# Cached sample keys of the third head group copied once through memory into 4 KB rows, and their reads issued from GpSimd

## The chip, the core and the metric

The kernel runs on one core of a Trainium2 chip. A core has a matrix engine (TensorE, PE in the profile), a vector engine (VectorE, DVE), a scalar engine (ScalarE, ACT), a general engine (GpSimd, POOL) and a queue engine (SyncE, SP) that mostly issues DMAs. Sixteen DMA engines move data between memory (HBM) and the on-chip memory. Each engine works through its own list of instructions in order and waits at semaphores. An instruction of one engine that has to wait holds up everything behind it on that engine, and nothing else.

The metric is the device time of one execution in microseconds (us). Lower is better.

## What is computed

One step of a decoder layer, for a prompt of 1024 tokens and for a sample group of 8 sequences with 8 new tokens each. The rest of the reference is a pooling branch, gates and a feed-forward part; the change concerns the attention of the sample tokens in the third of three head groups:

```python
ATTN_PATTERNS = ((128, 1), (512, 4), (2048, 16))     # (window, dilation) of the three groups of 4 heads
...
def dilated_attention_sample(q, k_full, v_full, dil, band):
    B, T, H, Dh = q.shape
    Lw = k_full.shape[1] - T
    idx = Lw + jnp.arange(T)[:, None] - jnp.arange(band + 1)[None, :] * dil
    valid = idx >= 0
    idxc = jnp.maximum(idx, 0)
    kg = k_full[:, idxc].astype(F32)
    vg = v_full[:, idxc].astype(F32)
    s = jnp.einsum('bthd,btjhd->bthj', q.astype(F32), kg) * (HEAD_DIM ** -0.5)
    p, lse = masked_softmax_stats(s, valid[None, :, None, :])
    return jnp.einsum('bthj,btjhd->bthd', p, vg), lse
```

With a dilation of 16 and 8 new tokens no two tokens of a sequence share a key. So each of the 64 sample tokens has 128 keys and values of its own in the cache, 16 rows apart.

## The kernel before

Products run in PE's passes over operands split into a high and a low part. Attention goes through the head groups in the order 2, 1, 0 (the third group first), and each group through 9 blocks: 8 of the prompt (0 to 7) and one of the sample tokens (8). For each block `qkv_part` multiplies the normed input by the weights of q, k and v. The order of PE's instructions is written out by hand; the order of the other engines' instructions is made by a scheduler that plays the program through with times of its own. `behind_pe` adds a wait on a product of PE, so that an instruction doesn't start ahead of its turn.

The norm of q and k of a block goes through four engines. ACT squares the product (L643 or L647), DVE or ACT sums the squares into `ms`, POOL adds a small constant (L650) and raises to the power -0.5 (L651, the result is `mr`), and ACT scales q and k by `mr` (L656, in `scale`). A few parts later PE transposes what was scaled (L672; the transposes are called `tqg2b`, `tqg1b`, `tqg0b` by the group). `smg0b` and its like are the scores, whose exponentials ACT takes in L699.

The own keys and values of the third group are not worked on by PE. `sample_own_keys` is a generator that takes one step with most parts of groups 1 and 0 (`own_step`). Its 128 partitions are the 64 sample tokens, twice: the first half of the 128 keys of each token in partitions 0 to 63, the second half in 64 to 127. It goes through 16 pieces of keys (`pck`) and then 16 of values (`pcv`); a piece has KPC = 4 keys of each partition, 512 KB. For a piece of keys POOL multiplies by the scaled q (`times`, L856, four instructions), and DVE sums over the head dimension into `sc` (L869). After the last one the softmax weights are made, and for a piece of values POOL multiplies by the weights and DVE adds the piece into `ss` (L894, L895).

Pieces are fetched by `piece` (L846): two DMAs of 64 partitions, each with 64 x 4 rows of 1 KB out of the cache. SP issues them. There are two buffers, so the DMA of the next piece but one waits until DVE has summed up the piece that holds its buffer. Every `times` waits also for PE's last product and for the last `mr` that was issued, so that a norm isn't queued behind it in the scheduler's order.

## Time and profile before

| | us |
|---|---|
| median of 3 timed runs | 1408.12 (1403.95 to 1409.54) |
| profiled execution | 1403.42 |
| its span, first to last instruction | 1401.6 |
| waits of POOL for key pieces (pck) | 24.5 in 10 |
| waits of POOL for value pieces (pcv) | 9.2 in 3 |
| POOL's products of key pieces, 64 | 47.4 |

The profile is of one execution. An engine's busy time is the time in which it had an instruction at work; its idle time is put down to what ended it. A share of 99% for PE says that the other engines cost time only where they make PE wait. In rows of the timeline the first number is the start in us from the span's start, the second the duration, and the bracket at the end holds the idle time ahead of it and what ended that. "SPq" and "POOLq" are the instructions with which SP and POOL issue DMAs and wait.

### The profile page before, as it was taken

How to read it: one execution, taken by the hardware profiler on the slowest of the kernel's cores; microseconds unless marked ns; L12 is line 12 of the kernel's file. 1: busy time of each engine (PE TensorE's matmuls, PEld its weight loads, DVE VectorE, ACT ScalarE, POOL GpSimd, SP SyncE). 2: the span in 40 equal slices, each digit the busy share in tenths (PEclk: the TensorE clock that was granted, in tenths of full speed). 3: DMA queues.
4: the chain of work that ended last, by engine and by line, in shares of the span. 5: the costliest groups of instructions: out<-in, count | busy, mean ns of one | idle time of the engine just before them, and what ended most of it. 6: DMA issues, size and time to landing. Idle time of an engine off the chain costs nothing.

```text
span 1401.6 us, 29306 instructions
## 1 busy us (share of the span) xinstructions
PE 1392.2 (99%) x11101; PEld 1342.7 (96%) x11101; DVE 954.3 (68%) x1714; ACT 754.5 (54%) x1778; POOL 236.2 (17%) x330
## 2 busy tenths in 40 slices
PE   9999999999999999999999999999999999999998
PEld 8988977887999999999999999999999999999998
DVE  7788744776776767875568677665665686664565
ACT  8557766687765323563336455555554544444443
POOL 0722266475500000000010000000000000000100
PEclk9999999999999999999999999999999999999999
DMA  6322788745477767965368668856758987777684
GB/s 215 117 90 102 220 228 215 216 127 144 120 254 232 253 216 250 319 227 179 130 203 285 227 221 269 269 200 210 249 189 287 325 272 261 234 243 231 206 260 168
DMA packets 184540, 303.57 MB, mean 217 GB/s; under 512 B 26567, under 2 KB 90509, under 8 KB 182350
## 3 DMA queue, kind: packets, MB, share of 16 engines
q1 hardware_dynamic: 181326, 258.04, 58.4%
q0 software_dynamic: 3072, 43.65, 9.8%
q8 instruction: 87, 1.43, 0.4%
q14 instruction: 55, 0.45, 0.1%
HBM read 231.55 MB, written 113.73 MB: 246 GB/s over the span
## 4 chain that ended last, share of the span: by engine, by line
PE 93%; DMA 2%; POOL 2%; DVE 1%; ACT 1%; issue 0%; SPq 0%; DVEq 0%; POOLq 0%
PE pz L1297 24%; PE pd L2075 24%; PE pg L1297 12%; PE ph L200 7%; PE pqk L200 5%; PE pab L1297 5%; PE pv L200 4%; PE a L328 3%; PE pq L200 1%; PE pk L200 1%; POOL pcv L856 1%; PE sg0b L689 1%; PE pog0b L722 1%; PE tpg0b L708 1%; POOL mr L651 0%; DMA ts_d<-ts 0%
## 5 line engine op out<-in xcount | busy, mean ns | idle before, releaser
L2075 PE MATMUL pd<-places 128*128 128x272 f32 x2688 | 331.7, 287 | 0.0
L2075 PEld LDWEIGHTS pd<-places 128*128 128x128 f32 x2688 | 331.6, 188 | 0.0
L116 ACT ACTIVATE places<-raw_d 128x544 fp32r<-128x544 f32 (+1 forms) x176 | 110.7, 646 | 162.7 <-DMA raw_d<-z_d 51.4
L117 DVE TENSOR_TENSOR places<-raw_d,places 128x544 fp32r<-128x544 f32 (+1 forms) x176 | 122.6, 712 | 92.4 <-ACT places L116 90.6
L2115 POOL DMA_DIRECT2D out_kv_sample_dram<-in_cache_kv_dram x96 | 47.2, 492 | 790.7 <-ACT places L116 580.9
L1297 PE MATMUL pz<-act,places 128*128 128x280 f32 (+1 forms) x1080 | 139.4, 287 | 0.0
L1297 PEld LDWEIGHTS pz<-act,places 128*128 128x128 f32 x1080 | 135.9, 188 | 0.0
L200 PE MATMUL ph<-act,places 128*128 128x280 f32 (+1 forms) x768 | 96.6, 287 | 0.0
L200 PEld LDWEIGHTS ph<-act,places 128*128 128x128 f32 x768 | 96.0, 188 | 0.1
L1297 PE MATMUL pg<-act,places 128*128 128x264 f32 (+1 forms) x576 | 75.6, 288 | 0.0
L1297 PEld LDWEIGHTS pg<-act,places 128*128 128x128 f32 x576 | 72.6, 188 | 0.6 <-issue 0.3
L1297 PE MATMUL pz<-places,apart 128*128 128x264 f32 (+1 forms) x528 | 67.9, 287 | 0.0
L1297 PEld LDWEIGHTS pz<-places,apart 128*128 128x128 f32 x528 | 66.6, 188 | 0.0
L200 PE MATMUL pqk<-places,act 128*128 128x512 f32 x240 | 60.6, 402 | 0.6 <-ACT qk L656 0.6
L1297 PE MATMUL pz<-act,apart 128*128 128x264 f32 (+1 forms) x456 | 59.2, 287 | 0.0
L1297 PEld LDWEIGHTS pz<-act,apart 128*128 128x128 f32 x456 | 57.5, 188 | 0.3 <-ACT e L1862 0.2
L200 PEld LDWEIGHTS pqk<-places,act 128*128 128x128 f32 x240 | 44.7, 192 | 10.5 <-ACT qk L656 0.8
L651 POOL TENSOR_TENSOR mr<-ms,mhalf 128x4 f32<-128x4 f32 (+2 forms) x39 | 52.9, 1356 | 3.1
L856 POOL TENSOR_TENSOR pck<-pck,qs 128x256 f32<-128x256 f32 x64 | 47.4, 774 | 29.1 <-DMA pck<-in_cache_kv_dram 24.5
L328 PE MATMUL a<-act,places 128*128 128x384 f32 (+1 forms) x288 | 50.3, 332 | 0.9 <-ACT act L306 0.4
L1297 PE MATMUL pab<-ab,places 128*128 128x264 f32 (+1 forms) x384 | 50.4, 286 | 0.0
L328 PEld LDWEIGHTS a<-act,places 128*128 128x128 f32 x288 | 47.5, 188 | 2.8 <-ACT act L306 1.2
(435 smaller groups left out, 2789.3 us busy)
## 6 DMA issues: line engine op xcount, KB each, us to landing
out_kv_sample_dram<-in_cache_kv_dram POOLq DMA_DIRECT2D x72, 480.0 KB, 4.9
raw_d<-z_d SPq DMA_DIRECT2D x112, 272.0 KB
z_d<-t SPq DMA_DIRECT2D x80, 272.0 KB
raw_d<-in_w_down_dram SPq DMA_DIRECT2D x80, 256.0 KB
raw_u<-in_w_up_dram SPq DMA_DIRECT2D x64, 256.0 KB
raw_qkv<-in_w_in_dram SPq DMA_DIRECT2D x36, 256.0 KB
pck<-in_cache_kv_dram SPq DMA_DIRECT2D x32, 256.0 KB
pcv<-in_cache_kv_dram SPq DMA_DIRECT2D x32, 256.0 KB
```

What stands on the lines that cost most here:

```text
L116: ins = s_.activation(dst_hi, src, AF.Copy)
L117: v_.tensor_tensor(dst_lo, src, dst_hi.bitcast(F32), op=ALU.subtract)
L200: last_mm[0] = t_.matmul(out, lhs(a, k), rhs(b, k), start=(j == 0), stop=(j == len(terms) - 1))
L328: last_mm[0] = t_.matmul(pts[m][:, :n], wt[:, a, kk, m * P:(m + 1) * P], act4[b][kk][:, :, part4(c)], start=(p == 0 and kk == 0), stop=(p ...
L651: last_norm[0] = g_.tensor_tensor(r[:n, :H], ms[:n, :H], mhalf[:n, :H], op=ALU.pow)
L689: t_.matmul(sc[e][:, hp, j * P:(j + 1) * P], qT[rows, hp, :], kT[rows, 2 + hp, :], start=True, stop=True)
L708: t_.transpose(tp[:, hp * nk + j, :], sms[e][:, hp, j * P:(j + 1) * P], ident)
L722: t_.matmul(po[e * HD:(e + 1) * HD, hp, :], vr[:, h * HD:(h + 1) * HD], pTs[e][:, hp * nk + j, :], start=(j == 0), stop=(j == nk - 1))
L856: ins = g_.tensor_tensor(out, *others, op=ALU.mult)
L1297: last_mm[0] = t_.matmul(out[c], lhs(*term), rhs(*term, c), start=(first and n == 0), stop=(n == len(terms) - 1), skip_group_check=not first)
L2075: last_mm[0] = t_.matmul(outs(chain[t], Q)[c], A[:, a, t * P:(t + 1) * P], Z[:, b, c], start=(fresh and f == 0 and n == 0), stop=(f == NG ...
L2115: ins = g_.dma_start(d, a)
```

## The change

It has two parts. First, during group 2 the keys of the 16 pieces are copied from the cache into a new array in memory, `own_d`: one tile for a piece, in which each of the 128 partitions has its four keys in one row of 4 KB. `own_rows` is a generator that issues two DMAs for a tile, 64 x 4 rows of 1 KB each, with a wait on PE's last product ahead of the first; one tile follows each of the prompt blocks' parts in group 2. `piece` then reads a piece of keys with one DMA of 128 rows of 4 KB. Values are read from the cache as before. Second, all of these DMAs are issued by POOL, where SP issued the reads of pieces before.

```diff
+    own_d = [dp.tile([P, KPC * 256], F32, name=f"own_d{n}") for n in range(16)]
...
     def piece(kv, j, name):
         t = rr(sp1, [P, KPC, 256], F32, name=f"pc{name}", tag="pc", bufs=2)
         src = i["cache_kv3"]
+        if not kv:
+            g_.dma_start(t.rearrange("p n d -> p (n d)"), own_d[j // KPC])
+            return t
         for hf in range(2):
             a = bass.AP(tensor=src.tensor, offset=src.offset + (64 * hf + j) * DIL[2] * NB * 512 + kv * 256,
                         ap=[[512, NT * NB], [DIL[2] * NB * 512, KPC], [1, 256]])
-            dma(t[64 * hf:64 * hf + 64], a)
+            g_.dma_start(t[64 * hf:64 * hf + 64], a)
         return t
+
+    def own_rows():
+        src = i["cache_kv3"]
+        row = DIL[2] * NB * 512
+        for n in range(16):
+            for hf in range(2):
+                a = bass.AP(tensor=src.tensor, offset=src.offset + (64 * hf + n * KPC) * row,
+                            ap=[[512, NT * NB], [row, KPC], [1, 256]])
+                behind_pe(g_.dma_start(own_d[n][64 * hf:64 * hf + 64].rearrange("p (n d) -> p n d", n=KPC), a))
+            yield
+
+    own_moves = own_rows()
...
                     feed()
+                    if g == 2 and b < 8:
+                        next(own_moves, None)
```

PE's instructions keep their order. The scheduler gives POOL, ACT, DVE and SP another one.

The first place is POOL in group 2, at blocks 1 and 2. In a row stand the line, the operation, and what is written from what; `ms` and `mr` are the two steps of the norm. Before:

```order
L650 TENSOR_TENSOR ms_1_1_1020<-ms_1_1_1020,stats 128x8
L651 TENSOR_TENSOR mr_1_1_1021<-ms_1_1_1020,mhalf 128x8
L650 TENSOR_TENSOR ms_2_1_1149<-ms_2_1_1149,stats 128x8
L651 TENSOR_TENSOR mr_2_1_1150<-ms_2_1_1149,mhalf 128x8
L650 TENSOR_TENSOR ms_3_1_1291<-ms_3_1_1291,stats 128x8
```

POOL in group 2 with the change, the same blocks:

```order
L860 DMA own_d_101<-in_cache_kv_dram 256x1x256 x2
L860 DMA own_d_102<-in_cache_kv_dram 256x1x256 x2
L651 TENSOR_TENSOR ms_1_1_1042<-ms_1_1_1042,stats 128x8
L652 TENSOR_TENSOR mr_1_1_1043<-ms_1_1_1042,mhalf 128x8
L860 DMA own_d_103<-in_cache_kv_dram 256x1x256 x2
L860 DMA own_d_104<-in_cache_kv_dram 256x1x256 x2
L651 TENSOR_TENSOR ms_2_1_1175<-ms_2_1_1175,stats 128x8
```

Between two norms stand two pairs of DMAs now; the first pair of the two waits for the product of v, the second for that of q and k, whose norm follows.

The second place is POOL in group 0, around the norm of block 1. Before:

```order
L651 TENSOR_TENSOR mr_0_1_3856<-ms_0_1_3855,mhalf 128x4
L856 TENSOR_TENSOR pcv_3823<-pcv_3823,sc 128x256 x4
L856 TENSOR_TENSOR pcv_3868<-pcv_3868,sc 128x256 x4
L856 TENSOR_TENSOR pcv_3945<-pcv_3945,sc 128x256 x4
L650 TENSOR_TENSOR ms_1_1_4061<-ms_1_1_4061,stats 128x8
L651 TENSOR_TENSOR mr_1_1_4062<-ms_1_1_4061,mhalf 128x8
L856 TENSOR_TENSOR pcv_4042<-pcv_4042,sc 128x256 x4
L856 TENSOR_TENSOR pcv_4167<-pcv_4167,sc 128x256 x4
L650 TENSOR_TENSOR ms_2_1_4212<-ms_2_1_4212,stats 128x8
```

POOL in group 0 with the change, from the same norm of block 0 on:

```order
L652 TENSOR_TENSOR mr_0_1_3888<-ms_0_1_3887,mhalf 128x4
L872 TENSOR_TENSOR pcv_3855<-pcv_3855,sc 128x256 x4
L850 DMA pcv_3900<-in_cache_kv_dram 64x4x256 x2
L850 DMA pcv_3977<-in_cache_kv_dram 64x4x256 x2
L872 TENSOR_TENSOR pcv_3900<-pcv_3900,sc 128x256 x4
L872 TENSOR_TENSOR pcv_3977<-pcv_3977,sc 128x256 x4
L651 TENSOR_TENSOR ms_1_1_4093<-ms_1_1_4093,stats 128x8
L850 DMA pcv_4074<-in_cache_kv_dram 64x4x256 x2
L652 TENSOR_TENSOR mr_1_1_4094<-ms_1_1_4093,mhalf 128x8
L850 DMA pcv_4199<-in_cache_kv_dram 64x4x256 x2
L872 TENSOR_TENSOR pcv_4074<-pcv_4074,sc 128x256 x4
L872 TENSOR_TENSOR pcv_4199<-pcv_4199,sc 128x256 x4
```

Three pairs of reads have come in between the norm of block 0 and that of block 1, the last of them between the two steps of the norm. Each pair waits in POOL's queue for DVE to be done with the buffer. From block 2 on two pairs stand in each block.

The third place is POOL at the start of group 1, from the first products of keys (`pck`) to the norm of block 1. Before:

```order
L856 TENSOR_TENSOR pck_2073<-pck_2073,qs 128x256 x4
L650 TENSOR_TENSOR ms_8_1_2198<-ms_8_1_2198,stats 64x4
L651 TENSOR_TENSOR mr_8_1_2199<-ms_8_1_2198,mhalf 64x4
L650 TENSOR_TENSOR ms_0_1_2252<-ms_0_1_2252,stats 128x4
L651 TENSOR_TENSOR mr_0_1_2253<-ms_0_1_2252,mhalf 128x4
L856 TENSOR_TENSOR pck_2172<-pck_2172,qs 128x256 x4
L856 TENSOR_TENSOR pck_2264<-pck_2264,qs 128x256 x4
L856 TENSOR_TENSOR pck_2324<-pck_2324,qs 128x256 x4
L650 TENSOR_TENSOR ms_1_1_2447<-ms_1_1_2447,stats 128x8
L651 TENSOR_TENSOR mr_1_1_2448<-ms_1_1_2447,mhalf 128x8
```

POOL at the start of group 1 with the change, from the norm of block 8 on:

```order
L652 TENSOR_TENSOR mr_8_1_2245<-ms_8_1_2244,mhalf 64x4
L872 TENSOR_TENSOR pck_2121<-pck_2121,qs 128x256 x4
L651 TENSOR_TENSOR ms_0_1_2298<-ms_0_1_2298,stats 128x4
L652 TENSOR_TENSOR mr_0_1_2299<-ms_0_1_2298,mhalf 128x4
L872 TENSOR_TENSOR pck_2219<-pck_2219,qs 128x256 x2
L845 DMA pck_2310<-own_d_101 128x1024
L872 TENSOR_TENSOR pck_2219<-pck_2219,qs 128x256 x2
L872 TENSOR_TENSOR pck_2310<-pck_2310,qs 128x256 x4
L845 DMA pck_2369<-own_d_102 128x1024
L651 TENSOR_TENSOR ms_1_1_2490<-ms_1_1_2490,stats 128x8
L652 TENSOR_TENSOR mr_1_1_2491<-ms_1_1_2490,mhalf 128x8
```

The norm of block 8 has moved ahead of the first products, that of block 1 stands behind three pieces where it stood behind four, and two reads have come in.

On ACT the scaling of q and k of a block, which waits for `mr`, has moved back by a few instructions in most blocks; in block 1 of group 0 it stands behind the exponentials of `smg0b`, where it stood ahead of them.

## The prediction

> **What bounds the kernel now.** I read the page's busy times first, then the digits of the 40 slices, the chain, the windows of the three attention stages, and last the waits of TensorE (PE).
>
> ```profile
> span 1401.6 us, 29306 instructions
> PE 1392.2 (99%) x11101; PEld 1342.7 (96%) x11101; DVE 954.3 (68%) x1714; ACT 754.5 (54%) x1778; POOL 236.2 (17%) x330
> POOL 0722266475500000000010000000000000000100
> DMA  6322788745477767965368668856758987777684
> PE 93%; DMA 2%; POOL 2%; DVE 1%; ACT 1%; issue 0%; SPq 0%; DVEq 0%; POOLq 0%
> ```
>
> PE leaves 1401.6 - 1392.2 = 9.4 us of its span unused. GpSimd (POOL) looks idle at 17%, but its digits say that it works in slices 2 to 11 alone, at up to seven tenths, and those are the slices the change touches (a slice is 35 us). The three stages, group 2, group 1 and group 0 of the attention, in that order:
>
> ```profile
> core 0: us, PE busy (x) PEld busy (x) DVE busy (x) ACT busy (x) POOL busy (x), PEclk, DMA share, GB/s
> 60.00:155.00 95.00, 95.00 (x660) 83.53 (x658) 76.09 (x183) 63.49 (x332) 30.00 (x31) 1.00 0.35 115
> 155.00:283.00 128.00, 125.07 (x1076) 104.60 (x1075) 76.11 (x202) 82.53 (x306) 68.33 (x94) 1.00 0.84 219
> 283.00:380.00 97.00, 96.94 (x799) 84.03 (x798) 67.06 (x187) 76.11 (x250) 62.42 (x86) 1.00 0.47 125
> ...
> PE pog1b L722 <- ACT pTg1b L711: 1.9, 1, 1.9
> PE pqk L200 <- ACT qk L656: 0.6, 1, 0.6
> PE tpg2b L708 <- ACT smg2b L699: 0.3, 1, 0.3
> ```
>
> The first rows are the windows, the last three PE's waits between 60 and 400 us. PE is full in all three stages, and waits 2.8 us in all. So **the change can win 2.8 us at most**. It can lose much more, since POOL makes the norm factors (mr) from which ScalarE (ACT) scales q and k, and PE transposes what is scaled. How late mr may come is read from pairs of rows: end of the scaling, start of the transposes of the same block.
>
> ```profile
> 87.70 1.75 ACT L656 ACTIVATE qk<-pqk,mr 128x64 f32<-128x64 f32 x8 [0.40 <-POOL mr L651]
> 94.15 0.60 PE L672 MATMUL tqg2b<-cst,qk 128*128 128x128 f32 x4
> ...
> 194.15 1.75 ACT L656 ACTIVATE qk<-pqk,mr 128x64 f32<-128x64 f32 x8 [3.18 <-POOL mr L651]
> 198.30 0.60 PE L672 MATMUL tqg1b<-cst,qk 128*128 128x128 f32 x4
> ...
> 307.36 1.75 ACT L656 ACTIVATE qk<-pqk,mr 128x64 f32<-128x64 f32 x8 [3.09 <-POOL mr L651]
> 311.95 0.60 PE L672 MATMUL tqg0b<-cst,qk 128*128 128x128 f32 x4
> 316.78 1.75 ACT L656 ACTIVATE qk<-pqk,mr 128x64 f32<-128x64 f32 x8 [0.18 <-POOL mr L651]
> 324.07 0.60 PE L672 MATMUL tqg0b<-cst,qk 128*128 128x128 f32 x4
> 376.25 0.66 PE L672 MATMUL tqg0b<-cst,qk 128*128 128x128 f32 x4
> ```
>
> The slack is 94.15 - 89.45 = 4.7 us in group 2, 198.30 - 195.90 = 2.4 in block 1 of group 1, 311.95 - 309.11 = 2.8 in block 1 of group 0, and 324.07 - 318.53 = 5.5 in its block 2. Blocks of group 0 follow each other every (376.25 - 311.95) / 5 = 12.86 us.
>
> **The price of a DMA on POOL.** The trace has POOL DMAs of one kind, 16 long rows each, and SP's DMAs of many kinds.
>
> ```profile
> L2115 POOL DMA_DIRECT2D out_kv_sample_dram<-in_cache_kv_dram x96: 488/488/717, 454.9 to 1335.0; - x96
> DMA to landing us min/median/max: 2.9/4.6/8.3
> ...
> q0 software_dynamic: 3072, 43.65, 9.8%
> ...
> L846 SPq DMA_DIRECT2D pcv<-in_cache_kv_dram x32: 595/610/1452, 262.8 to 366.0; - x32
> ...
> 60.32 0.33 SPq L127 DMA_DIRECT2D raw_qkv<-in_w_in_dram  x1
> ```
>
> Lower end: 0.49 us, the POOL row as it is. Upper end: in proportion to packets. 3072 / 96 = 32 packets cost 0.49, and 256 rows are at least 256 packets, so 8 x 0.49 = 3.9 us. SP, which generates in another way, pays 0.61 for this very pattern and 0.33 for a plain one, 1.85 times; 0.49 x 1.85 = 0.90. I take **1.0 us** for 256 rows (nearest to SP's ratio, a little above it since POOL's row had only 16) and 0.7 for the 128 rows of a key piece, between 0.49 and 0.9. All of this is an estimate; the chances below carry its doubt.
>
> By the Trainium skill, "DMA: Bandwidth & Descriptors", section "Anatomy of one DMA — SWDGE (gpsimd) path", a lot of descriptors can be emitted before their number costs anything; the price would then stay at 0.49, the result of the first rival. No POOL DMA of many rows is in this trace, so nothing here bears it out or refutes it.
>
> **The change part by part.**
>
> *Moves to own_d, group 2.* 16 pairs, 32 DMAs, 32 us: POOL goes from 30 to 62 of 95. Each pair waits for the product whose norm comes next, and stands ahead of ms and mr.
>
> ```profile
> 83.31 0.22 ACT L647 ACTIVATE qk<-pqk 128x64 f32<-128x64 f32 x1 [2.13 <-PE pqk L200]
> ...
> 85.14 0.45 POOL L650 TENSOR_TENSOR ms<-ms,stats 128x8 f32<-128x8 f32 x1 [9.89 <-ACT qk L647]
> ```
>
> After the product ACT squares for 85.14 - 83.31 = 1.8 us before POOL can begin, and POOL idles 9.9 us until then. A pair of 2.0 us makes mr 0.2 late, of 4.7 allowed: **0**. At 3.9 it would be 6.0 late, 1.3 us a block. The transfers add 8.4 MB: at the 219 GB/s for a share of 0.84 of the second window that is 38 us at 0.84, or 0.34 of 95 us on top of 0.35. There is room.
>
> *Key reads, group 1.* 16 x 0.7 = 11 us: POOL goes to about 80 of 128. Two reads, 1.4 us, come ahead of mr of block 1, where 2.4 are allowed and one piece of four products less stands in front: **0**. SP loses 64 issues of 0.61 us, and waits that go with them; SP is not in the chain, so I credit nothing there. The 0.6 us wait for qk goes, because mr of block 8 now stands ahead of the first products: **-0.6** (0 to -2.8).
>
> *Value reads, group 0.* 14 of the 16 pairs fall behind 283 us: 28 us, POOL at 90 of 97. Here it gets tight.
>
> ```profile
> L856 POOL TENSOR_TENSOR pcv<-pcv,sc 128x256 f32<-128x256 f32 x64 | 42.5, 695 | 22.2 <-DMA pcv<-in_cache_kv_dram 9.2 <-DVE natt L601 3.0 <-PE pv L200 2.9
> ...
> 296.92 2.33 POOL L856 TENSOR_TENSOR pcv<-pcv,sc 128x256 f32<-128x256 f32 x4 [2.15 <-DVE sel L1227]
> 302.28 2.83 POOL L856 TENSOR_TENSOR pcv<-pcv,sc 128x256 f32<-128x256 f32 x4 [3.03 <-DVE natt L601]
> 305.06 0.20 POOL L650 TENSOR_TENSOR ms<-ms,stats 128x8 f32<-128x8 f32 x1
> 305.34 1.98 POOL L651 TENSOR_TENSOR mr<-ms,mhalf 128x8 f32<-128x8 f32 x1
> ...
> 312.94 1.26 SPq L846 DMA_DIRECT2D pcv<-in_cache_kv_dram  x2
> 317.71 2.33 POOL L856 TENSOR_TENSOR pcv<-pcv,sc 128x256 f32<-128x256 f32 x4 [0.96 <-DMA pcv<-in_cache_kv_dram]
> 318.28 1.27 SPq L846 DMA_DIRECT2D pcv<-in_cache_kv_dram  x2
> 324.52 2.49 POOL L856 TENSOR_TENSOR pcv<-pcv,sc 128x256 f32<-128x256 f32 x4 [4.49 <-DMA pcv<-in_cache_kv_dram]
> ```
>
> Block 1: three pairs, 6.0 us, now stand between mr of block 0 and mr of block 1 (the order's rows). POOL idled 2.15 + 3.03 = 5.2 us there. If all of it absorbs issues, mr is 0.8 late and the slack of 2.8 covers it; if none does, because each pair waits for VectorE (DVE) to have added up the piece that holds its buffer and the products then wait for the landing, it is 6.0 late and PE stands 3.2. I take the middle, **+1.6**.
>
> Blocks 2 to 6: two pairs a block. Data land some 4.25 us after the issue (314.20 to 317.71 is 3.5, 319.55 to 324.52 is 5.0). One round on POOL: pair 2.0, mr 1.7, pair 2.0, landing 0.55, products 2.35, landing 1.35, products 2.35, ms 0.2: 12.5 us against PE's 12.86: **0**, with 5.5 of slack behind it.
>
> Sum: 0 + 0 - 0.6 + 1.6 + 0 = **+1.0 us**. On the profiled execution, 1403.4 us (1.8 beyond its span), that makes 1404.4; the median of the three timed runs is 1408.1, 4.7 above that execution, and I forecast on it: **1409 us**.
>
> **Rivals.**
> 1. *Flat issue price.* At 0.49 us the three pairs ahead of mr are 3.0, less than the idle 5.2. No stall, and between 0.6 and 2.8 us are won: about **1407**.
> 2. *POOL becomes the bound, slower.* At 1.7 us a DMA, block 1 adds 6 x 0.7 = 4.2 to the stall, 5.8. The round becomes 6.8 + 1.7 + 2.35 + 1.9 + 2.35 + 0.2 = 15.3, 2.4 beyond PE's pace in each of five blocks, 12 less the slack of 5.5: 6.7. With -0.6 that is +12: **1420**. It decides from about 1.5 us a DMA, where the same sum gives 7. For it: POOL is already at 62 of 97, and each read makes norm and products wait in one queue behind DVE. Against: SP's ratio of 1.85 and the 12.5 of 12.86. At 3.9 us it would be some 80 us.
> 3. *DVE's copies hold the issue back.*
>
> ```profile
> 326.04 1.88 DVE L601 CAST natt<-act 128x256 fp32r<-128x256 f32 x4
> ```
>
> If a pair of each block had to wait out these copies, the round is 14.4 us: 1.5 over in five blocks less 5.5 is 2, and block 1 takes 1.9 more: +5, **1413**. In the trace POOL's products once began just as such copies ended (3.03), and no DMA fell beside them. The Trainium skill, "SBUF — State Buffer", section "SBUF: two separate sides", says that GpSimd cannot write descriptors while a DVE copy of this kind holds the shared port.
> 4. *It does not do what it says:* 4 KB rows shorten what POOL waits for keys, and that wait is not on PE's path. This is inside the forecast. A result faster by over 7 us would need most of PE's 9.4 idle us, of which 2.8 lie in these stages.
>
> **How the numbers follow.** Chances: the forecast 0.46, flat price 0.15, POOL as bound 0.28, copies 0.08, something faster that I don't see 0.03. 0.5% is 7 us, about what a measurement of this kernel can tell from no change. Beyond +7 fall the second rival, 0.06 of the forecast (its upper ends) and 0.02 of the copies: slower 0.36. Faster 0.03 + 0.01 = 0.04. Same 0.60. The range goes from 1402 (all of PE's 2.8 won on a low run) to 1424 (the second rival a little above 1.7 us); above it lies some 0.12.
>
> **What would show it.** POOL's DMA row with 256 packets, at 0.8 to 1.3 us, settles the price. POOL busy near 62, 80 and 90 in the three windows, and the pairs of scaling and transposes with slack left except in block 1 of group 0, show the sum right. PE waits for qk or smg0b of more than 3 us between 283 and 400 us, or blocks further apart than 12.86, show the second rival. Wrong would be my reading if PE lost time in group 2, where I see none, or if the value pieces came so late that DVE stood behind them ahead of the softmax masks.

## The result, and the profile after

The changed kernel takes 1416.94 us (median of 6 runs, 1415.47 to 1419.86) where the kernel before takes 1406.45 us in the runs beside it (6 runs, 1403.95 to 1409.54). The ratio is 1.0077, with a 95% interval of 1.0066 to 1.0088: slower by some 10.5 us. The prediction had 1409 us as the likeliest time and 1402 to 1424 as its range; "slower by over 0.5%" had 0.36. One of the six executions of a kernel below (the change with both orders put back) was a slow one, 1938 us at a mean clock of 0.65, and its ratio leaves it out.

From the page of the profile after, the lines that answer to those of before (span, busy time of each engine, chain):

```profile
span 1416.0 us, 29304 instructions
...
PE 1397.5 (99%) x11101; PEld 1345.5 (95%) x11101; DVE 965.4 (68%) x1714; ACT 752.5 (53%) x1778; POOL 281.8 (20%) x410
...
PE 85%; DMA 6%; POOL 3%; DVE 2%; issue 1%; ACT 1%; SPq 0%; DVEq 0%; POOLq 0%; ACTq 0%
```

PE's unused time rose from 9.4 us to 1416.0 - 1397.5 = 18.5, and its share of the chain fell from 93% to 85%; what came in are DMA, POOL and DVE. PE's busy time rose too, by 5.3 us for the same products. The spans are 14.4 us apart, 3.9 more than the medians, since the profiled execution of before is a short one; landmarks below are from the two profiles and add up to the 14.4.

The windows of the three stages after, with the columns as before (busy time of PE, PEld, DVE, ACT, POOL, then granted clock, DMA share, GB/s), and behind them PE's waits between 60 and 400 us (total, times, longest):

```profile
60.00:155.00 95.00, 93.10 (x638) 81.46 (x637) 74.52 (x177) 59.38 (x319) 44.63 (x62) 1.00 0.60 187
155.00:283.00 128.00, 122.44 (x1032) 101.85 (x1032) 75.00 (x196) 80.21 (x302) 78.32 (x110) 0.99 0.72 221
283.00:380.00 97.00, 92.93 (x737) 78.58 (x736) 67.56 (x175) 70.42 (x235) 74.67 (x106) 1.00 0.47 120
```

```profile
PE pog2b L723 <- ACT pTg2b L712: 2.7, 1, 2.7
PE sg0b L690 <- ACT pTg0b L712: 1.2, 1, 1.2
PE tqg0b L673 <- ACT qk L657: 1.2, 1, 1.2
PE sg0b L690 <- DVE p L988: 1.1, 1, 1.1
PE sg2b L690 <- DVE qkTg2b L676: 1.0, 1, 1.0
```

Every stage leaves PE 2 to 6 us idle, the largest wait being 2.7. POOL's busy time is below the forecast in group 2 and group 0 (44.6 and 74.7, forecast 62 and 90), and at it in group 1 (78.3, forecast 80), because its DMAs are cheaper than I took them to be:

```profile
L2133 POOL DMA_DIRECT2D out_kv_sample_dram<-in_cache_kv_dram x96 | 47.1, 491 | 794.0 <-ACT places L116 583.8 <-ACT gapart L116 105.6 <-ACT apart L116 104.5
L850 POOL DMA_DIRECT2D pcv<-in_cache_kv_dram x32 | 20.5, 641 | 9.2 <-DVE sc L885 7.4 <-DVE ss L911 1.0 <-DVE md L699 0.8
L860 POOL DMA_DIRECT2D own_d<-in_cache_kv_dram x32 | 19.6, 619 | 33.0 <-PE pqk L200 21.7 <-PE tqg2b L673 4.4 <-PE tpg2b L709 2.6
L845 POOL DMA_DIRECT2D pck<-own_d x16 | 9.5, 594 | 12.4 <-PE tpg2b L709 5.9 <-DVE sc L885 5.5 <-DVE p L988 1.0
```

In these groups of POOL's DMAs the second number behind the bar is the mean in ns: 491 for 16 rows, 594 for 128, 619 and 641 for 256. So a price near to the first rival's, and a time near to the second's.

### Where PE falls behind

The best ruler is PE's transposes `tqg2b`, `tqg1b` and `tqg0b`, which come in the same order in all kernels. The table has how much later than in the kernel before some of them start in each profile; its columns are named by the start in before (the first and one of the last in group 2; the first and the last of group 1; the first and the last of group 0), and the last one is the span. The difference of two neighbouring columns is what is lost on the way from one to the other. Each row is one profile. How far two executions of one kernel differ by it was not measured; but the five runs whose edit leaves group 2 to itself (issuer alone, all on SP, values held, price alone, norms in order) all lose 0.0 between the first two columns, so that part of the ruler repeats.

| profile | 83.11 | 142.64 | 182.81 | 279.63 | 296.00 | 386.98 | span |
|---|---|---|---|---|---|---|---|
| the change | 0.3 | 2.2 | 5.7 | 7.4 | 8.1 | 13.6 | 14.4 |
| moves alone | 0.2 | 2.2 | 7.9 | 6.4 | 6.4 | 6.2 | 7.8 |
| moves of one row alone | 0.4 | 2.7 | 3.5 | 4.3 | 4.3 | 4.0 | 5.8 |
| issuer alone | 0.0 | 0.0 | 6.3 | 5.4 | 6.2 | 10.9 | 10.8 |
| change, values on SP | 1.0 | 2.3 | 4.5 | 6.0 | 6.8 | 7.4 | 7.4 |
| all on SP | 0.0 | 0.0 | 5.5 | 3.3 | 3.3 | 3.6 | 5.0 |
| values held on SP | 1.1 | 1.1 | 2.9 | 4.1 | 4.1 | 21.4 | 21.1 |
| issue price alone | 0.2 | 0.2 | 0.4 | 5.4 | 5.4 | 7.9 | 8.6 |
| all on SP, norms in order | 0.6 | 0.6 | 3.4 | 0.8 | 1.0 | 1.4 | 1.0 |
| moves alone, both orders put back | 0.2 | 1.5 | 6.6 | 7.9 | 7.9 | 8.1 | 7.7 |
| change, both orders put back | 0.6 | 2.8 | 6.8 | 8.7 | 9.6 | 14.4 | 14.6 |
| the same, first keys on SP | 0.8 | 4.6 | 9.5 | 9.1 | 10.1 | 14.7 | 15.5 |
| all on SP, norms first | 0.2 | 1.0 | 1.2 | -1.3 | -1.3 | -0.9 | -0.2 |

The change loses 0.3 us ahead of group 2's first transposes, 1.8 in group 2, 3.5 at its end, 2.4 on the way through group 1 (1.7 of it up to the last transposes there), 5.5 in group 0 and 0.8 behind it: 14.4, but for rounding.

**The end of group 2.** Rows of the timeline after, by engine (start, duration, and in the bracket the idle time and what ended it), and then slices of 1 us with the granted clock as the third number from the right:

```profile
162.11 1.17 POOL L845 DMA_DIRECT2D pck<-own_d  x2 [5.89 <-PE tpg2b L709]
...
163.04 0.33 SPq L127 DMA_DIRECT2D raw_qkv<-in_w_in_dram  x1
...
169.54 0.63 ACT L116 ACTIVATE places<-raw_qkv 128x512 fp32r<-128x512 f32 x1 [6.09 <-DMA raw_qkv<-in_w_in_dram]
170.07 0.35 ACT L712 COPY pTg2b<-tpg2b 128x256 f32<-128x256 f32 x1
...
170.48 0.96 PE L723 MATMUL pog2b<-pTg2b,v 128*64 128x128 f32 x6 [2.70 <-ACT pTg2b L712]
```

```profile
170.00:171.00 1.00, 0.52 (x5) 0.52 (x6) 0.97 (x3) 0.96 (x4) 0.00 (x0) 0.84 1.02 421
171.00:172.00 1.00, 1.00 (x7) 0.67 (x5) 0.97 (x3) 0.00 (x0) 0.00 (x0) 0.50 1.01 387
172.00:173.00 1.00, 1.00 (x7) 1.00 (x6) 0.49 (x2) 0.80 (x3) 0.00 (x0) 0.50 1.06 384
173.00:174.00 1.00, 1.00 (x7) 1.00 (x7) 0.96 (x3) 1.00 (x5) 0.75 (x2) 0.50 1.12 396
```

In the kernel before the same places look like this in the timeline:

```profile
162.62 1.32 ACT L116 ACTIVATE places<-raw_qkv 128x512 fp32r<-128x512 f32 x2 [2.68 <-DMA raw_qkv<-in_w_in_dram]
...
166.96 1.32 SPq L846 DMA_DIRECT2D pck<-in_cache_kv_dram  x2
```

Before, the first reads of keys stood in SP's queue behind its last loads of weights (`raw_qkv`) and started at 166.96. POOL's queue has no such loads in it: it issues the two reads at 162.11, 1 MB, just ahead of the load of 163.04, which is the one that ACT takes up at 169.54 (loads and ACT's steps come in one order, and both are the 22nd of 36). From its issue until ACT goes on that load takes 6.5 us; before, the same load was issued at 158.66 and taken up at 162.62, 4.0 later. So it comes later for two reasons: 4.4 us by its issue, where PE itself is 2.9 behind, and 2.5 by its landing. ACT is 6.1 us idle, and the copy pTg2b that PE needs stands behind that on ACT. PE waits 2.7 us, and for 3.4 us after it (170.67 to 174.09) the granted clock is 0.5; by the slices that is 0.52 x 0.16 + 3 x 0.5 = 1.6 us of PE's work more.

The Trainium skill, "TensorE: Matmul & The Clock Gate", section "Part 1: The HAM clock gate (the "warmup" mystery)", puts PE's clock at one half after an idle window of about 3.4 us, and back at full after a busy one of that length. The trace agrees with the half and with the length of the way back; but a shorter idle time was enough here: 2.7 us, in 3.41 us before the drop of which PE was busy for 0.71.

**Group 0.** The longest round of value pieces after, from POOL's, DVE's, ACT's and PE's timelines:

```profile
327.06 1.25 POOL L850 DMA_DIRECT2D pcv<-in_cache_kv_dram  x2
328.33 1.67 POOL L652 TENSOR_TENSOR mr<-ms,mhalf 128x8 f32<-128x8 f32 x1
329.95 1.29 POOL L850 DMA_DIRECT2D pcv<-in_cache_kv_dram  x2
334.64 2.33 POOL L872 TENSOR_TENSOR pcv<-pcv,sc 128x256 f32<-128x256 f32 x4 [3.40 <-DMA pcv<-in_cache_kv_dram]
338.73 3.11 POOL L872 TENSOR_TENSOR pcv<-pcv,sc 128x256 f32<-128x256 f32 x4 [1.76 <-DMA pcv<-in_cache_kv_dram]
341.80 0.20 POOL L651 TENSOR_TENSOR ms<-ms,stats 128x8 f32<-128x8 f32 x1
...
337.01 0.69 DVE L910 TENSOR_TENSOR pcv<-pcv 128x512 f32<-128x512 f32 x1 [4.75 <-POOL pcv L872]
...
342.70 0.22 ACT L752 ACTIVATE ce<-ce 128x24 f32<-128x24 f32 x1 [4.57 <-DVE ce L751]
...
342.93 0.37 PE L690 MATMUL sg0b<-qkTg0b,qkTg0b 64*128 64x128 f32 x1 [1.09 <-DVE p L988]
```

The pair issued at 327.06 has landed by 334.64, 6.3 us after its issue ended at 328.31. That is not the common case: over the 32 value reads the median from issue to landing is 3.9 us, and these land late beside three loads of weights (`raw_ga`) that SP issues from 325.32, with the DMA share at 1.0 or more from 327 to 336 us. POOL's products wait for it, DVE stands 4.75 us behind the products to add the piece up, ACT stands 4.57 behind DVE, and PE waits for what DVE and ACT have left undone (`p`, pTg0b). The round takes 341.94 - 327.06 = 14.9 us where PE's pace is 12.86, and PE loses 1.7 us up to the next transposes.

The larger loss, 2.6 us between the transposes of blocks 4 and 5, comes in no long round (352.63 to 361.68) but again by order. Rows of after:

```profile
359.70 0.69 DVE L910 TENSOR_TENSOR pcv<-pcv 128x512 f32<-128x512 f32 x1 [3.72 <-POOL pcv L872]
...
361.50 0.51 ACT L700 ACTIVATE smg0b<-smg0b,md 128x256 f32<-128x256 f32 x1 [2.72 <-DVE md L699]
...
369.70 1.75 ACT L657 ACTIVATE qk<-pqk,mr 128x64 f32<-128x64 f32 x8 [2.07 <-POOL mr L652]
371.30 0.64 ACT L712 COPY pTg0b<-tpg0b 128x512 f32<-128x512 f32 x1
...
371.99 0.37 PE L690 MATMUL sg0b<-qkTg0b,qkTg0b 64*128 64x128 f32 x1 [1.20 <-ACT pTg0b L712]
```

DVE stands 3.7 us behind POOL's products ahead of the softmax masks (`md`), and ACT 2.7 behind the masks. Later POOL's mr comes late as well, ACT idles 2.1 us for it, and the copy pTg0b stands behind that scaling in ACT's order: PE waits 1.2 us. The products that PE makes meanwhile out of `natt`, which DVE and ACT copy, take 3.96 us where they took 3.05 before, 0.9 more.

### The profile page after: what moved, and what is told of

It reads as the page before. It is cut to its first block, busy times and chain, and to the rows that moved or that the text cites. A ratio compares the mean times of both kernels' runs of the same rounds, so it can differ in the third digit from the quotient of the medians.

```text
span 1416.0 us, 29304 instructions
## 1 busy us (share of the span) xinstructions
PE 1397.5 (99%) x11101; PEld 1345.5 (95%) x11101; DVE 965.4 (68%) x1714; ACT 752.5 (53%) x1778; POOL 281.8 (20%) x410
## 4 chain that ended last, share of the span: by engine, by line
PE 85%; DMA 6%; POOL 3%; DVE 2%; issue 1%; ACT 1%; SPq 0%; DVEq 0%; POOLq 0%; ACTq 0%
PE pd L2093 23%; PE pz L1315 22%; PE pg L1315 12%; PE ph L200 7%; PE pab L1315 5%; PE a L329 3%; PE pqk L200 2%; PE pv L200 2%; DMA pcv<-in_cache_kv_dram 2%; POOL pcv L872 2%; DMA ts_d<-ts 2%; PE pq L200 1%; DMA raw_qkv<-in_w_in_dram 1%; PE pk L200 1%; POOL mr L652 1%
## 5 line engine op out<-in xcount | busy, mean ns | idle before, releaser
L872 POOL TENSOR_TENSOR pck<-pck,qs 128x256 f32<-128x256 f32 x64 | 47.4, 771 | 16.2 <-DMA pck<-own_d 10.9
```

The lines of the kernel that those rows point to most:

```text
L872: ins = g_.tensor_tensor(out, *others, op=ALU.mult)
```

## The experiments

Each ratio is against the kernel before, with a 95% interval; 0.1% is 1.4 us.

### One part of the change at a time

Moves alone: `piece` reads from the cache by SP again.

```diff
-        if not kv:
-            g_.dma_start(t.rearrange("p n d -> p (n d)"), own_d[j // KPC])
-            return t
...
-            g_.dma_start(t[64 * hf:64 * hf + 64], a)
+            dma(t[64 * hf:64 * hf + 64], a)
```

> The moves to own_d stay (32 DMAs on POOL in group 2), but the pieces of keys and values are read from the cache by SP, as before; own_d is written and not read. Theory G (the loss has two places, and one is group 2: the moves, by their traffic or by their place in POOL's queue, make PE late): +4 to +7 us against before, with PE's last transposes of group 2 (tqg2b of block 7) 4 to 6 us later than before, and no further loss in groups 1 and 0. Theory V (the loss comes from reads on POOL's queue alone, and what is seen in group 2 is another order of work that is made up later): 0 to +2 us. My prediction's own step said 0.

Measured: 1.0052 (1.0034 to 1.0070). The loss in group 2 is there, 1.9 us between the first two columns, though not the 4 to 6 that I expected; then PE waits 4.8 us for qk at the start of group 1, which the change doesn't.

Issuer alone: the kernel before, with `g_.dma_start` for `dma` in `piece`, and no own_d.

> No own_d and no moves; the reads of keys and values come from the cache as before, in two DMAs of 1 KB rows each, but POOL issues them. Theory G: group 2 is as before to 0.5 us, and the loss is that of groups 1 and 0, +5 to +9 us, most of it in group 0. Theory V: +9 to +12 us, the whole loss. My prediction's own steps said +1.6 for value reads in block 1 of group 0 and 0 after it. The price of a DMA of 256 rows into on-chip memory should again be about 0.63 us.

Measured: 1.0052 (1.0032 to 1.0071). Group 2 is as before to 0.0, group 0 loses 10.9 - 6.2 = 4.7 us. Each part alone costs half a per cent, and the whole 0.77%: they don't add up, since at the start of group 1 each loses something in another way.

Values on SP: the change, with `dma` for the value reads alone.

> The change as it is, but the reads of values are issued by SP again; moves and key reads stay on POOL. Theory G: the loss of group 0 goes, that of group 2 stays: +4 to +7 us. Theory V: 0 to +2 us. If value reads aren't the cause in group 0: still +9 to +12.

Measured: 1.0050 (1.0033 to 1.0068). The loss of group 0 falls from 5.5 to 0.6 us.

All on SP: moves, key reads out of own_d and value reads issued by `dma`.

```diff
-            g_.dma_start(t.rearrange("p n d -> p (n d)"), own_d[j // KPC])
+            dma(t.rearrange("p n d -> p (n d)"), own_d[j // KPC])
...
-            g_.dma_start(t[64 * hf:64 * hf + 64], a)
+            dma(t[64 * hf:64 * hf + 64], a)
...
-                behind_pe(g_.dma_start(own_d[n][64 * hf:64 * hf + 64].rearrange("p (n d) -> p n d", n=KPC), a))
+                behind_pe(dma(own_d[n][64 * hf:64 * hf + 64].rearrange("p (n d) -> p n d", n=KPC), a))
```

> The layout of the change with SP as the issuer of everything: the moves, the reads of keys out of own_d and the reads of values. The traffic is that of the change, POOL's queue is that of before. If the loss in group 2 is traffic: +4 to +7 us, with PE's last transposes of group 2 late by 4 to 6. If it is the place of the moves in POOL's queue: within 1.5 us of before, unless SP's own queue, which issues 32 DMAs more at some 0.6 us and waits for PE ahead of them, holds up the loads and stores of group 2; then the waits for raw_qkv and ts_d show that.

Measured: 1.0015 (1.0000 to 1.0030). With the same traffic group 2 loses nothing (0.0). PE has one large wait, at the start of group 1, and the rows of POOL's timeline say why:

```profile
PE pqk L200 <- ACT qk L657: 4.6, 1, 4.6
```

```profile
175.60 2.81 POOL L872 TENSOR_TENSOR pck<-pck,qs 128x256 f32<-128x256 f32 x4 [4.80 <-DVE sc L890]
178.36 0.34 POOL L651 TENSOR_TENSOR ms<-ms,stats 128x4 f32<-128x4 f32 x2
178.66 1.98 POOL L652 TENSOR_TENSOR mr<-ms,mhalf 128x4 f32<-128x4 f32 x2
```

POOL stands in the first key products, and the two norms behind them (of blocks 8 and 0) have come out in another order: block 0's mr is first, and ACT scales block 8, for which PE waits, after block 0 and two exponentials.

### What it is in group 2 and in group 0

Moves of one row, each DMA cut from 64 partitions to 1:

```diff
-                            ap=[[512, NT * NB], [row, KPC], [1, 256]])
-                behind_pe(g_.dma_start(own_d[n][64 * hf:64 * hf + 64].rearrange("p (n d) -> p n d", n=KPC), a))
+                            ap=[[512, 1], [row, KPC], [1, 256]])
+                behind_pe(g_.dma_start(own_d[n][64 * hf:64 * hf + 1].rearrange("p (n d) -> p n d", n=KPC), a))
```

> As the run with the moves alone, but each move copies one partition of its 64 (4 rows of 1 KB), so own_d stays mostly unwritten; it isn't read. 32 DMAs are still issued by POOL at the same places, with the same waits for PE, at some 0.49 us each where they took 0.6; nearly all traffic is gone. Theory T (the traffic, set off by POOL just ahead of the stores of ts, lands on the same DMA engines and holds those stores up, and DVE waits for them): ts_d lands within 3.5 us again, DVE's wait for it falls from 9.3 to about 4 us, and PE's transposes of group 2, blocks 2 to 6, are at most 0.5 us later than before, where they were 2.2 with the full moves. Theory P (the place in POOL's queue, in front of the norm): still 2 us late. In total, the wait of 4.8 us for qk at the start of group 1, which I put down to another order of two norms, should stay: +4 to +6 by T, +7 by P.

Measured: 1.0027 (1.0010 to 1.0044). Nearly all traffic is gone, and group 2 loses 2.3 us, no less than with it. Theory T falls. The wait for qk at the start of group 1, which I expected to stay at 4.8 us, is 0.9 here: such waits come and go with the scheduler's order. Four rows cost POOL 549 ns in the mean of 32 DMAs (median 520).

Values held: the kernel before, with each value read on SP waiting for the last product of the piece ahead (`piece` gives its two DMAs a wait on `last`).

```diff
-            if j + KPC < 64:
-                loaded.append(piece(1, j + KPC, f"v{j + KPC}"))
             for n in range(KPC):
                 tv = t[:, n].rearrange("p (h d) -> p h d", h=4)
-                times(tv, tv, sc[:, j + n, :].unsqueeze(2).to_broadcast([P, 4, HD]))
+                last = times(tv, tv, sc[:, j + n, :].unsqueeze(2).to_broadcast([P, 4, HD]))
+            if j + KPC < 64:
+                loaded.append(piece(1, j + KPC, f"v{j + KPC}", last))
```

> The kernel before, with value reads on SP, each held until POOL's products of the piece ahead of it are done, as POOL's own order holds them in the change. POOL issues nothing. Theory O (order: what costs time in group 0 is that a read issued by POOL starts only after POOL's next products, some 2 us after its buffer came free, so that the piece lands late, POOL's products are late, and DVE and ACT, in their order, after them): blocks of group 0 further apart, +3 to +6 us between the first and the last transposes of group 0 against before, and about that in total. Theory P (the time in which POOL issues, 1.25 us a pair, ahead of mr): 0 to +1 us.

Measured: 1.0117 (1.0088 to 1.0147), 17.3 us of it in group 0, with two stretches there in which PE's clock is at one half. Reads that start later cost PE time with POOL issuing nothing, but far more than the change loses: a read held on SP also holds what stands behind it in SP's queue. The sign speaks for theory O, the size can't be used.

Price alone: two DMAs more on POOL for each value piece.

```diff
                 loaded.append(piece(1, j + KPC, f"v{j + KPC}"))
+                for hf in range(2):
+                    a = bass.AP(tensor=i["cache_kv3"].tensor, offset=i["cache_kv3"].offset + (64 * hf + j) * DIL[2] * NB * 512,
+                                ap=[[512, 1], [DIL[2] * NB * 512, KPC], [1, 256]])
+                    ins = g_.dma_start(own_x[j // KPC, hf:hf + 1].rearrange("p (n d) -> p n d", n=KPC), a)
+                    behind_pe(ins, adds[-1] if adds else None)
```

> The kernel before, with value reads on SP as before, and with two more DMAs on POOL for each value piece, each of one partition (4 rows of 1 KB) into an array that nothing reads. They wait for DVE's sum as a read would, and stand in POOL's order where the change has its reads. They take POOL 2 x 0.49 us, most of the 1.25 us of a real pair, and add hardly any traffic. Theory P: +3 to +6 us in group 0. Theory O: 0 to +1.5 us. If both come to about half, the loss is the sum of the two.

Measured: 1.0025 (1.0009 to 1.0041), 2.5 us of it between the first and the last transposes of group 0 (a wait of 3.8 us for pTg1b at the end of group 1 costs more, and the change doesn't have it). So about half of the 4.6 to 5.5 us of the four profiles with value reads on POOL is the time and the place of the issue; the other half, by subtraction alone, comes with the reads themselves.

### Orders put back

Norms in order: all on SP, and each ms waits for the mr before it.

```diff
-            g_.tensor_tensor(ms[:n, :H], ms[:n, :H], xeps[go][:n, col:col + 1].to_broadcast([n, H]), op=ALU.add)
+            ins = g_.tensor_tensor(ms[:n, :H], ms[:n, :H], xeps[go][:n, col:col + 1].to_broadcast([n, H]), op=ALU.add)
+            if last_norm[0] is not None:
+                behind_pe(ins, last_norm[0])
```

> As the run with everything on SP, with one wait more: POOL's step ms of each norm waits for the mr before it, so that the norms stay in the order of the kernel before. At the start of group 1 that puts the norm of block 8 ahead of that of block 0 again, where the scheduler had let both ms go first. If the 4.6 us that PE waited there for qk, and the stretch after it in which the granted clock was 0.5, come from that order: the wait falls to 1 us or less, no stretch of lower clock is left, and the time falls by 4 to 6 us, to 2 us below before. If they come from something else (keys landing late, SP's queue): no change against that run, +2 to +3 over before.

Measured: 0.9989 (0.9972 to 1.0006), 2.6 permille below the run without it. The wait fell from 4.6 to 2.4 us, not to 1, and a stretch of some 3 us at a clock near 0.5 stayed: block 8's norm is first now, but still behind key products that wait for their DMA.

Both orders put back: the wait above, and DVE's window sum `win` (L477) waiting for the last sum of `ts` (L533) ahead of it in the program; for the moves alone, and for the whole change.

```diff
-                v_.tensor_tensor(v[:, 2], v[:, 2], v[:, 0], op=ALU.add)
+                last_ts[0] = v_.tensor_tensor(v[:, 2], v[:, 2], v[:, 0], op=ALU.add)
...
-            behind_pe(v_.tensor_tensor(nxt[:, lo:], cur[:, lo:], cur[:, lo - w:LS - w], op=ALU.add))
+            ins = v_.tensor_tensor(nxt[:, lo:], cur[:, lo:], cur[:, lo - w:LS - w], op=ALU.add)
+            behind_pe(ins)
+            if last_ts[0] is not None:
+                behind_pe(ins, last_ts[0])
```

> The moves alone (all of their traffic, issued by POOL in group 2; pieces read from the cache by SP), with two orders put back to those of the kernel before by waits of an engine on itself: DVE's window sums (win) wait for the last sum of ts that stands ahead of them in the program, and POOL's ms waits for the mr before it. The run with the moves cut to one row had lost as much in group 2 as the full moves, so traffic is not the cause there. Theory S (the scheduler's other order of DVE, which puts the store of ts 2 to 3 us later, is the cause): blocks 2 to 6 of group 2 at most 0.7 us later than before, where they were 2.2; the wait for qk at the start of group 1 at 1 us or less; in total 0 to +2.5 us where the moves alone had +7. Theory P (POOL's issue ahead of the norm is the cause): still 2 us late in group 2, +3 to +4 in total.

> The change as it is, with the same two orders put back. By S, what is lost in blocks 2 to 6 of group 2 goes (2.2 us), and what is left is the wait of 2.7 us for pTg2b with its stretch at half clock, and the loss of group 0 (5.5 us): +6 to +9 us against before, where the change had +10.5. By P: still +10 to +11.

Measured: 1.0051 (1.0035 to 1.0066) for the moves alone, 1.0094 (1.0074 to 1.0114) for the change. Neither gains. In group 2 (between the first two columns) the moves on POOL lose 1.3 us where they lost 1.9, but the wait on `ts` has a cost of its own there: with all on SP and both orders put back (the last run below) group 2 loses 0.8 us. With DVE's order put back POOL's moves thus lose 0.5 more than SP's, without it 1.9 more. That points to the order, and isn't clean enough to call it shown: the whole change with both orders put back loses 2.2 there.

First keys on SP: the change with both orders put back, and the first two key pieces read by SP.

```diff
-            g_.dma_start(t.rearrange("p n d -> p (n d)"), own_d[j // KPC])
+            (dma if j < 2 * KPC else g_.dma_start)(t.rearrange("p n d -> p (n d)"), own_d[j // KPC])
```

> As the change with the two orders put back, but SP issues the first two reads of keys, behind its loads of raw_qkv. Theory C (collision: POOL's queue lets these two reads of 512 KB start at 162 us, beside the loads of raw_qkv, which land 3 us later; ACT waits for them 6 us, PE for ACT 2.7, and the clock falls to a half): PE's wait for pTg2b goes, ACT's longest wait for raw_qkv falls from 6 to about 3 us, 3 to 5 us less than the run beside it that keeps these reads on POOL. If the late loads come from something else (their own issue, the moves): no difference to that run.

Measured: 1.0080 (1.0066 to 1.0095), no clear gain on the run beside it. In ACT's and PE's waits (ACT's between 150 and 190 us):

```profile
ACT places L116 <- DMA raw_qkv<-in_w_in_dram: 6.8, 5, 2.9
ACT qk L662 <- DVE sc L890: 2.8, 1, 2.8
```

```profile
PE pqk L200 <- ACT qk L662: 2.6, 1, 2.6
```

The collision is gone as theory C has it: ACT's longest wait for raw_qkv is 2.9 us where it was 5.7 in the run beside it, the load that took 6.2 us from issue until ACT goes on in that run takes 3.3, and PE's wait for pTg2b isn't there. But keys that are read later land later, POOL stands in their products ahead of block 8's norm, and PE waits 2.6 us for qk instead, again with the clock at 0.5 behind it. A wait took the place of the one removed. In group 2 this run also has a stretch at half the clock (105.99 to 109.41, 1.4 us lost) that the run beside it was spared, which hides a part of what the edit gains.

Norms first: all on SP, both orders put back, and the products of the first key piece one step later.

```diff
+            if j == 0:
+                yield
             for n in range(KPC):
                 times(t[:, n], t[:, n], qs[:, :256])
-            yield
+            if j != 8 * KPC:
+                yield
```

> Everything on SP with the orders put back, and the products of the first key piece one step later, so that POOL has the norms of blocks 8 and 0 of group 1 ahead of them. In the run before that one (orders put back, first products ahead) PE still waited 2.4 us for qk there, since POOL stood in those products until the keys had landed, and the clock fell to 0.53 and 0.62. If that is so, the wait falls below 0.6 and no stretch at lower clock is left: 3 to 4 us less, 1401 to 1403, which would be faster than both kernels. If the later products make the last ones late in group 0, or something else ends the wait: no gain, 1404 to 1408.

Measured: 0.9987 (0.9976 to 0.9997), 1403.88 us beside 1406.08. PE's waits from 60 to 420 us are these three, and no slice up to the last 4 us has a clock below 1.00:

```profile
PE pqk L200 <- ACT qk L662: 0.7, 1, 0.7
PE pl L511 <- DVE ext L486: 0.5, 1, 0.5
PE sg2b L695 <- ACT am L514: 0.3, 1, 0.3
```

It ends 2 us ahead of the kernel before, whose waits in these stages were 2.8 us, and is the only one whose interval lies below 1; from the run with the norms in order (0.9989) it can't be told apart. The move of the keys into long rows needn't cost anything, then: on SP, with the norms ahead of the first products. Whether it is worth anything is open, since the kernel before was not run with its norms first; these 2 us may be the order's alone.

## Why the prediction was right or wrong

The time lies in the range, but the likeliest case, no difference, was wrong: the sum of +1.0 us met 10.5. That the time is in the range is luck in the main: the range was drawn up to 1424 for the second rival, and the price that this rival needs isn't there. By its steps:

*What bounds the kernel.* Right. PE was full, there was little to win and much to lose.

*The price of a DMA on POOL.* Mis-sized: 1.0 us taken for 256 rows, 0.62 to 0.64 measured; 0.7 taken for 128 rows, 0.59 measured. The rule of the first rival (the Trainium skill, "DMA: Bandwidth & Descriptors", "Anatomy of one DMA — SWDGE (gpsimd) path", by which many descriptors can be emitted before their number costs) holds in this trace: 16 times the rows cost 1.3 times the time. The upper end of 3.9 us took 256 rows for at least 256 packets. The pages count 3072 packets on POOL's queue before and 8192 with the issuer alone, whose 64 DMAs thus make 80 each; 128 rows of 4 KB make 144, and are cheaper than the 80. So the price goes neither by packets nor by rows. It decided nothing. At the cheap price the forecast would have been lower still, 1407, and the kernel was slower than that by ten.

*Moves to own_d, group 2: 0.* Failed; 1.8 us. The part of it on traffic ("There is room") was right: all of the traffic on SP loses 0.0, next to none of it on POOL 2.3. The part on mr was right too, no wait for mr stands there. I looked only at the engine that got the new instructions. What came late was DVE: in group 2 its last sum of `ts` stands behind the softmax masks now, the store ts_d is issued at 95.38 where it was 92.82, and DVE waits for that store before it can copy qkTg2b, for which PE waits 1.0 us. Rows of before, and then of after:

```profile
92.82 0.55 SPq L533 DMA_DIRECT2D ts_d<-ts  x1
...
96.21 1.36 DVE L524 TENSOR_TENSOR ts<-act,act 128x544 f32<-128x544 f32 x2 [1.08 <-DMA ts_d<-ts]
...
100.04 0.41 DVE L675 COPY qkTg2b<-tqg2b 128x256 f32<-128x256 f32 x1
```

```profile
95.38 0.55 SPq L534 DMA_DIRECT2D ts_d<-ts  x1
...
100.99 1.36 DVE L525 TENSOR_TENSOR ts<-act,act 128x544 f32<-128x544 f32 x2 [2.83 <-DMA ts_d<-ts]
...
102.91 0.71 PE L690 MATMUL sg2b<-qkTg2b 64*128 64x128 f32 x8 [1.00 <-DVE qkTg2b L676]
```

The scheduler's order of DVE changed with the moves on POOL. In the traces of all on SP and of the issuer alone, which lose 0.0, DVE's instructions from 62 to 130 us come in the order of before, and in the four runs with moves on POOL and no order put back (the change, moves alone, one row, values on SP), which lose 1.3 to 2.3, they don't. But order and issue came and went together in these runs, so that the order is the whole cause is not shown, as said above. The store also takes longer, 5.6 us until DVE goes on where it was 96.21 - 92.82 = 3.4 before, and 5.2 with the moves of one row; what lengthens it stays open.

*Key reads, group 1: 0, and -0.6.* The -0.6 came: PE has no wait for qk at the start of group 1 with the change, and the norm of block 8 ahead of the products is what made it so. The 0 failed. "SP loses 64 issues of 0.61 us ... I credit nothing there" saw SP's queue only as time. It was also an order: it kept the first reads behind the loads of raw_qkv. Most of the 3.5 us lost at the end of group 2 is that: PE is 2.9 behind ahead of its wait for pTg2b, 5.9 with the wait, 7.5 with the half clock, and comes back to 5.7 around two waits of 0.3 and 0.6 (for smg2b and qk) that only the kernel before has. That is more than any term of the sum, and no rival had it. A further 1.7 us were lost in the middle of group 1, in small waits.

*Value reads, group 0.* Block 1: +1.6 forecast, 1.0 measured (8.15 to 9.17 at its transposes). The mechanism was that of the forecast, with a term added: before, mr ended 4.6 us ahead of the transposes (307.32 and 311.95); now it ends at 318.75, 1.2 us ahead of where they would begin but for their wait (321.11 - 1.20). That is 3.5 later, within the 0.8 to 6.0 taken. ACT takes it up 1.0 later still, behind exponentials.

```profile
316.53 2.22 POOL L652 TENSOR_TENSOR mr<-ms,mhalf 128x8 f32<-128x8 f32 x1
...
321.11 0.96 PE L673 MATMUL tqg0b<-cst,qk 128*128 128x128 f32 x4 [1.20 <-ACT qk L657]
```

Blocks 2 to 6: **0** forecast, 4.9 measured (9.17 to 14.04), 1.7 of it up to block 3's transposes and 2.6 up to block 5's; this step failed. The round of 12.5 us was built from a landing of 4.25 us; in the long round above two pairs took 6.3 and 7.5 (331.24 to 338.73), so POOL waits 3.4 and 1.8 for them where I had 0.55 and 1.35, though its issues are 1.5 us cheaper. The landing was not mis-sized on the mean (the median is 3.9), and neither was the round: 11.8, 14.9 and 10.7 (315.26, 327.06, 341.94, 352.63) average 12.5. What failed is the step from a mean round to no loss: PE doesn't get back in short rounds what it lost in a long one, and 2.6 us went in a short one, by the order of DVE and ACT. And the slack of 5.5 for mr was not that of the path that bound, which goes over DVE's masks and ACT's copies: the prediction's last sentence, that it would be wrong "if the value pieces came so late that DVE stood behind them ahead of the softmax masks", is what happened. DVE's waits for POOL's value products between 283 and 400 us grew from 8.6 to 13.6:

```profile
DVE pcv L910 <- POOL pcv L872: 13.6, 7, 4.8
```

*The rivals.* The second had the right side and the right stage, and reached 1420 by a price of 1.7 us that isn't there. What makes POOL's queue a bound is not the price but that a read waits its turn behind products and norms, and they behind its landing. The third (DVE's copies hold the issue back) is not seen: the issues of pairs in group 0 take 1.23 to 1.30 us, with DVE's copies beside some of them.

## What to carry to other kernels

A queue that a DMA is moved out of was also an order: before moving a read to an engine with an emptier queue, ask what will start earlier, which loads it will run beside, and which engine waits for those. Take the slack of every engine that waits in order behind the moved work, not only of the value that it makes, and follow the waits round by round, since a mean round hides them. And where a scheduler lays out the other engines, compare their orders as well: a moved DMA can cost in a stage where its own time and traffic cost nothing.

## What the runs showed of the hardware

POOL's DMAs have a nearly flat price: in the mean 549 ns for 4 rows of 1 KB (median 520), 491 for 16 rows, 594 for 128 rows of 4 KB (144 packets), 619 to 641 for 256 rows of 1 KB (80 packets).

PE's granted clock fell to 0.5 after waits of less than 3 us: after 2.7 in the change, 2.1 with values on SP, 2.4 with the norms in order, 1.8 with the first keys on SP (105.99). A wait of 1.9 in the kernel before was not followed by it, and neither was one of 2.6 with the issuer alone, so the length of the wait doesn't settle it.

The stretches in these stages last 3.41 us or twice that, and where one profile has two, they start a whole number of times 3.41 us apart: 27 times (184.47 and 276.63, moves alone with both orders put back), 9 times (326.31 and 357.03, values held), 24 times (105.99 and 187.91, first keys on SP). That looks like a fixed grid, and PE's busy share of the whole step ahead seems to count: it was 0.21 in the change (167.26 to 170.67) and 0.48 with the first keys on SP (102.58 to 105.99), while the waits of 2.6 and 1.9 that were spared fall on two steps each, of which the emptier has 0.52 and 0.55. One step of 0.45 was spared too (moves alone, 178.97 to 182.38), so the limit is not shown.

A stretch of 3.4 us cost PE 1.4 to 1.6 us of its work on top of the wait, and one of 6.8 us 2.2 to 3.2 (2.2 behind the 4.6 us with all on SP), in busy time that a list of waits doesn't show.
